# Gate copies on ScalarE, six PSUM banks for the second mixer, an MLP input scaled by ScalarE, and a later head norm

## The chip, the core and the metric

The kernel runs on one core of a Trainium2 chip. Its engines are TensorE (PE: matmuls and their weight loads), VectorE (DVE), ScalarE (ACT), GpSimd (POOL) and SyncE (SP, which issues the large DMAs). Each runs its own instructions in order and waits for others by semaphores. Operands lie in SBUF; matmul results go to PSUM, eight banks of 128 x 512 float32, from where VectorE and ScalarE read them. The metric is the device time of one execution in microseconds; the time before is the median of three runs.

## The reference

x has 256 tokens of width 1024. Three layers follow each other, each a mixer and a feed-forward part, all with an RMS norm ahead and a residual behind:

```
layer 0: x += even_mix(norm(x));  x += peer_ffn(norm(x))
layer 1: x += fox_mix(norm(x));   x += peer_ffn(norm(x))
layer 2: x += mix2(norm(x));      x += conv_gated_mlp(norm(x))
```

- peer_ffn: from q = h @ wq (8 heads, two halves of 128) the scores against 128 keys per half; the top 16 of each, the top 16 of their sums, a softmax over these. That makes 8 x 16 chosen experts out of 16384 for each token, each with a gate. act = gelu(h . u[expert]); the result is the sum of gate * act * v[expert].
- fox_mix: causal attention of 16 heads with normed q and k and a learned forget bias; o @ w_out.
- mix2: windowed attention of 8 heads with sinks, beside a spatial gating branch; both gated by sigmoids, merged and projected.
- conv_gated_mlp: z = h @ w_up, a causal convolution of three taps over the tokens, (silu(gate) * val) @ w_down.

## The kernel before, in words

Activations are kept transposed (128 features x 256 tokens, eight such blocks in xT). Each float32 weight block of 128 x 1024 comes by one DMA (w_raw), is rounded by ScalarE (`w_hi`, L337, in `Stream._hi`) and its rest is made by VectorE (`w_lo` = w_raw - w_hi, L353, in `Stream._split`). `mm3` (L454) makes one product out of three matmuls: hi x hi, hi x lo and lo x hi. Every block of work asks for its weights with `st.get()`, which also splits the block that stands two further on (look=2): so w_hi and w_lo of a later block stand in the program right ahead of the work that follows on the present one.

The expert layers (`peer`, twice) treat all 16384 experts densely in 128 blocks c of 128 experts. For each c: 24 matmuls make the up product in a PSUM bank (`pu`), ScalarE applies Gelu into a large tile X (L1271). In the same loop the gates are built (`gates`), four tokens at a step (GT = 4, so 64 steps), as a background generator that gets a turn after each block. One step s consists of

- `onehots(s)`: ScalarE makes a one-hot of the first key (four Abs, L1168, and a Relu, L1174), VectorE one of the second key and three products of it with parts of the gate (L1170, L1173);
- `products(s-1)`: twelve small matmuls into one PSUM bank `g`; two banks (2 and 3) take turns;
- `put(s-2)`: the gates of four tokens are brought into X. Blocks that have their activations already (c below `done["c"]`) are multiplied (L1190, two instructions, as X is two tiles), the others just get the gate copied in (L1192). When an activation comes later, ScalarE writes Gelu to `gl` (L1274) for the tokens that have gates already, and VectorE multiplies it into X (L1275).

The order is fixed in the program: after block c's up product come the Gelu, then one gate step. The library that records the program adds the semaphore waits that the accesses of tiles need, per tile in SBUF and per bank in PSUM. Background turns are counted by constants and not by measured time. After the 128 blocks the down products (`pv`) follow, with X as the moving operand.

The attention layer (`odd`) projects q and k in sixteen blocks. `quad(b)` (L1516) norms two heads' q and k: sums of squares by small matmuls (`qn_ps`), reciprocal roots, a broadcast by TensorE (`qn_rb`), products on VectorE. The generators in `flow` move one step on after each projection. When the last quad has run, eight `pair_chain`s are queued, one for two heads: logits (`lg`), softmax, transposes (`pt`), the product with v (`po`), and a split into y_hi (ScalarE) and y_lo (VectorE), after which `ready` names the pair. `attend` puts a block of projection work between their steps: the eight blocks of v, then six row blocks of the output projection (`rows`, one for each ready pair), then the last two.

`banks(j, a, l, o)` says which PSUM banks the projections (pj) and the small products (pa) take in turn; `acc(i)` is bank 4 + i. `mix2` begins with six projections (k, v, four q), then the value accumulators `va` in banks 4 and 5.

In `mlp` the first six pairs of up projections use h = xT * gain without the norm's factor, which VectorE multiplies in behind them (`zi`); from i = 6 on they use `hn`, the fully normed input. `normed()` makes it, one of eight blocks k at a flow step: room = xT * rb * gain on POOL (L1749, L1750), hn_hi on ScalarE (L1752), hn_lo on POOL (L1754).

Of the kernel before, what the change touches and what calls it, by code (L numbers as in the profile page):

```python
# [15 lines left out]
AF = mybir.ActivationFunctionType  # L16
OP = mybir.AluOpType
# [361 lines left out]
def body(ctx: ExitStack, tc: tile.TileContext, a, out, phases=(0, 6)):  # L379
    nc = tc.nc  # L380
# [21 lines left out]
    def banks(j, a_, l=(0,), o=(0,)):  # L402
        pj.set(j)
        pa.set(a_)
        pl.set(l)
        po.set(o)
# [6 lines left out]
    xT = base.tile([P, KD, S], F32, name="xT")  # L413
# [13 lines left out]
    def col(name, i=0, n=1):  # L427
        at, w = COLS[name]
        assert i + n <= w
        return cols[:, at + i:at + i + n]  # L430
# [44 lines left out]
    rb = base.tile([P, S], F32, name="rb")  # L475
# [514 lines left out]
    def peer(l):  # L990
        banks((0, 1, 4, 5), (2, 3))
        with ExitStack() as es:
# [50 lines left out]
            room = X(0, KD)  # L1043
# [109 lines left out]
            GT = 4  # L1153
            def gates():
                full = [P, GT // 2, P, 2]

                def pairs(t):

                    return t.rearrange("p (a b) -> p a b", b=2).unsqueeze(2).to_broadcast(full)

                def onehots(t0):


                    o = [t[:, i] for t in [tp.tile([P, 2, GT * P], BF16, name=t, tag=t) for t in ("oa", "ob")]
                         for i in range(2)]
                    two = [t.rearrange("p (a n b) -> p a n b", a=GT // 2, b=2) for t in o[1:]]
                    for i in range(GT):
                        nc.scalar.activation(o[0][:, i * P:(i + 1) * P], iota, AF.Abs,  # L1168
                                             bias=ne1T[:, t0 + i:t0 + i + 1])
                    nc.vector.tensor_tensor(two[2], iota2.unsqueeze(1).to_broadcast(full), pairs(e2b[:, t0:t0 + GT]),  # L1170
                                            op=OP.is_equal)
                    for part in range(3):
                        nc.vector.tensor_tensor(two[part], two[2], pairs(g3[:, part, t0:t0 + GT]), op=OP.mult)  # L1173
                    nc.scalar.activation(o[0], o[0], AF.Relu, bias=1.0, scale=-1.0)  # L1174
                    return o

                def products(o):
                    g = pa("g")
                    for i in range(GT):
                        for part in range(3):  # L1180
                            w = o[1 + part].rearrange("p (a n b) -> p a n b", a=GT // 2, b=2)[:, i // 2, :, i % 2]
                            mm(g[:, i * P:(i + 1) * P], o[0][:, i * P:(i + 1) * P], w,
                               i + part == 0, i == GT - 1 and part == 2)
                    return g

                def put(t0, g):
                    gt = g.rearrange("p (t c) -> p c t", t=GT)
                    c = done["c"]
                    for lo, hi, x in spans(0, c):
                        nc.vector.tensor_mul(x[:, :, t0:t0 + GT], gt[:, lo:hi], x[:, :, t0:t0 + GT])  # L1190
                    for lo, hi, x in spans(c, NCH):
                        nc.vector.tensor_copy(x[:, :, t0:t0 + GT], gt[:, lo:hi])  # L1192
                    done["t"] = t0 + GT

                n = S // GT
                hot, prod = {}, {}
                for s in range(n + 2):
                    if s < n:
                        hot[s] = onehots(s * GT)
                    if 0 <= s - 1 < n:  # L1200
                        prod[s - 1] = products(hot.pop(s - 1))
                    if s - 2 >= 0:
                        put((s - 2) * GT, prod.pop(s - 2))
                    yield G_COST
# [221 lines left out]
    def odd():  # L1426
        banks((4, 5, 6, 7), (0, 1, 2, 3))
        with ExitStack() as es:
# [85 lines left out]
            ready = set()  # L1514

            def quad(b):  # L1516
                yield from rms_heads(lambda b: qk[:, b], qz, lambda b: sq[:, slot(b)], [b, 8 + b, b + 1, 9 + b], [gq, col("odk"), gq, col("odk")], tp, bd64)
                if b == 6:
                    preload(AF.Exp)
                    for bb in range(8):  # L1520
                        pending.append(pair_chain(bb, (2 * bb, 2 * bb + 1), tp, qz, qk[:, 8 + bb], y, bias,
                                                  lambda hd: [cq[:, tb, hd:hd + 1] for tb in range(2)],
                                                  lambda hd: None, lambda hd: hd * 64, vn, ready))
# [36 lines left out]


    def mix2():
        banks((4, 5, 6, 7), (0, 1, 2, 3))
        with ExitStack() as es:
            sp = es.enter_context(tc.tile_pool(name="m2", bufs=1))
            st.extend(sp, 2, 3, 46)
# [166 lines left out]
    def mlp():  # L1733
        banks((0, 1, 4, 5, 6, 7), (2, 3))
        with ExitStack() as es:
            sp = es.enter_context(tc.tile_pool(name="ml", bufs=1))
            st.extend(sp, 3, 3, 66)
            tp = es.enter_context(tc.tile_pool(name="ml_t", bufs=2))
            room = sp.tile([P, KD, S], F32, name="room")
            hn = (sp.tile([P, KD, S], F32R, name="hn_hi"), sp.tile([P, KD, S], F32R, name="hn_lo"))  # L1740
            m = (sp.tile([P, NFF, S], F32R, name="m_hi"), sp.tile([P, NFF, S], F32R, name="m_lo"))

            zz = {}

            def normed():

                for k in range(KD + 2):
                    if k < KD:
                        nc.gpsimd.tensor_tensor(room[:, k], xT[:, k], rb, op=OP.mult)  # L1749
                        nc.gpsimd.tensor_scalar(room[:, k], room[:, k], col("ffn2", k), None, op0=OP.mult)  # L1750
                    if 0 <= k - 1 < KD:
                        nc.scalar.activation(hn[0][:, k - 1], room[:, k - 1], AF.Copy)  # L1752
                    if k - 2 >= 0:
                        nc.gpsimd.tensor_tensor(hn[1][:, k - 2], room[:, k - 2], hn[0][:, k - 2].bitcast(F32),  # L1754
                                                op=OP.subtract)
                    yield

            def conv(i, e, ps, scaled):

                if scaled:  # L1760
                    zi = tp.tile([P, S], F32, name="zi", tag="zi", bufs=3)
                    nc.vector.tensor_mul(zi, ps[:, :S], rb)
                    ps = zi
                    yield
                b = i + e * NFF
                z = tp.tile([P, S], F32, name="z", tag="z", bufs=8)
                w = lambda j: col("cw2", 3 * b + j)
                nc.scalar.activation(z, ps[:, :S], AF.Identity, scale=w(2), bias=col("cb2", b))
                for j in (1, 0):
                    s = 2 - j  # L1770
                    nc.vector.scalar_tensor_tensor(z[:, s:], ps[:, :S - s], w(j), z[:, s:], op0=OP.mult, op1=OP.add)
                zz[i, e] = z
                if e:
                    flow.add(gated(i))

            def gated(i):
                sg = tp.tile([P, S], F32, name="sg", tag="sg", bufs=4)
                nc.scalar.activation(sg, zz.pop((i, 0)), AF.Silu)
                yield
                nc.vector.tensor_mul(sg, sg, zz.pop((i, 1)))  # L1780
                yield
                nc.scalar.activation(m[0][:, i], sg, AF.Copy)
                yield
                nc.vector.tensor_sub(m[1][:, i], sg, m[0][:, i].bitcast(F32))

            def up_out(i, e, ps):
                flow.add(conv(i, e, ps, i < 6))

            proj2(h, lambda e, ps: up_out(0, e, ps))
            for i in range(1, NFF):  # L1790
                for e in range(2):
                    ps = pj("up")
                    proj_t(h if i < 6 else hn, ps[:, :S], then=lambda i=i, e=e, ps=ps: up_out(i, e, ps))
                    if (i, e) == (1, 0):
                        flow.add(normed())
                    flow.step()
            flush()
            flow.drain()
            w = None
            for n in range(KD):  # L1800
                ps = pj("dn")
                for i in range(NFF):
                    f = n * NFF + i
                    if f % 8 == 0:
                        w = st.get()
                    mm3(ps[:, :S], [t[:, (f % 8) * P:(f % 8 + 1) * P] for t in w], [t[:, i] for t in m],
                        i == 0, i == NFF - 1)
                nc.vector.tensor_add(xT[:, n], xT[:, n], ps[:, :S])  # L1808
                nc.sync.dma_start(out[:, n], xT[:, n])
# [38 lines left out]
```

## Time and profile before

| | before |
|---|---|
| median of 3 runs (lowest, highest) | 2348.55 us (2344.61, 2349.74) |
| the profiled execution | 2352.38 us, span 2350.6 |
| TensorE busy | 2315.8 us (99%) |
| VectorE busy | 1723.3 us (73%) |
| ScalarE busy | 1357.8 us (58%) |
| POOL busy | 93.6 us (4%) |
| mean granted TensorE clock | 0.994 |

Stages by time: the even mixer to about 155 us, the first expert layer to 1010 (its gates from 372 to 605), attention to 1155, the second expert layer to 1995 (gates from 1354 to 1587), the second mixer to 2150, the MLP to the end. A timeline row gives start, length, engine, line, operation and tiles, and in brackets the engine's idle time before it with what ended it. Matmuls are pipelined: the next one starts 0.12 us after a 256-wide one, though each row is 0.28 long, so TensorE's lost time is read from the distance of starts. The other engines also start an instruction a little before the one ahead has ended. Times of single instructions come from one profiled execution.

### The profile page before, as it was taken

The page shows a single profiled execution, that of the slowest core. Times are in us where ns is not written, and L with a number is a line of the kernel's source. Part 1 is how long each engine was busy: PE and PEld are TensorE (multiplying, and loading weights), DVE is VectorE, ACT ScalarE, POOL GpSimd, SP SyncE. Part 2 cuts the span into 40 slices and gives each one's busy share as a digit, 9 for nine tenths or more (in the row PEclk, how much of TensorE's full clock was granted, in tenths as well). Part 3 has the DMA queues.
Part 4 walks back from the last instruction along what each step waited for, and adds up shares of the span by engine and source line. Part 5 has one row for each costly group of instructions (what it writes and reads, how often), then busy time and mean ns, then how long its engine had stood idle before and what let it go on. Part 6 is the DMA issues. An engine that isn't in the chain of part 4 may idle for free. (4 is left out here: it accounts for less than half of the span.)

```text
span 2350.6 us, 48812 instructions
## 1 busy us (share of the span) xinstructions
PE 2315.8 (99%) x19664; PEld 2268.3 (97%) x19664; DVE 1723.3 (73%) x3656; ACT 1357.8 (58%) x2480; POOL 93.6 (4%) x107
## 2 busy tenths in 40 slices
PE   8999999999999999999999999999999999999999
PEld 7889999999999999998899999999999999999999
DVE  6668999999755555566699899996555555667983
ACT  6226448888544444455564588884444445555762
POOL 4100000000000000010000000000000000002300
PEclk9899999999999999999999999999999999999999
DMA  6114654444555666553256544446556565645553
GB/s 214 54 63 163 193 185 156 149 145 140 174 185 185 206 186 184 178 193 117 89 165 190 186 145 147 144 142 188 185 185 206 185 185 161 210 137 177 181 182 123
DMA packets 106626, 386.82 MB, mean 165 GB/s; under 512 B 11959, under 2 KB 13272, under 8 KB 106016
## 3 DMA queue, kind: packets, MB, share of 16 engines
q1 hardware_dynamic: 104976, 377.99, 50.7%
q0 software_dynamic: 1136, 5.32, 0.7%
q8 instruction: 154, 2.52, 0.4%
q14 instruction: 72, 0.59, 0.1%
q10 hardware_dynamic: 288, 0.40, 0.1%
HBM read 383.40 MB, written 1.05 MB: 164 GB/s over the span
## 5 line engine op out<-in xcount | busy, mean ns | idle before, releaser
L353 DVE TENSOR_TENSOR w_lo<-w_raw,w_hi 128x1024 fp32r<-128x1024 f32 x710 | 866.4, 1224 | 383.9 <-ACT w_hi L337 382.3
L337 ACT ACTIVATE w_hi<-w_raw 128x1024 fp32r<-128x1024 f32 x710 | 745.6, 1054 | 432.6 <-PE pv L452 348.0
L452 PE MATMUL pu<-h_hi,w_hi 128*128 128x256 f32 x2048 | 586.9, 287 | 0.0
L452 PE MATMUL pu<-h_lo,w_hi 128*128 128x256 f32 x2048 | 575.2, 281 | 0.0
L452 PE MATMUL pu<-h_hi,w_lo 128*128 128x256 f32 x2048 | 574.5, 281 | 0.0
L452 PE MATMUL pv<-h_hi,w_hi 128*128 128x256 f32 x1888 | 530.4, 281 | 0.0
L452 PE MATMUL pv<-h_lo,w_hi 128*128 128x256 f32 x1888 | 530.4, 281 | 0.0
L452 PE MATMUL pv<-h_hi,w_lo 128*128 128x256 f32 x1888 | 530.4, 281 | 0.0
L452 PEld LDWEIGHTS pu<-h_lo,w_hi 128*128 128x128 f32 x2048 | 386.4, 189 | 0.0
L452 PEld LDWEIGHTS pu<-h_hi,w_lo 128*128 128x128 f32 x2048 | 385.8, 188 | 0.0
L452 PEld LDWEIGHTS pu<-h_hi,w_hi 128*128 128x128 f32 x2048 | 385.5, 188 | 0.0
L452 PEld LDWEIGHTS pv<-h_hi,w_lo 128*128 128x128 f32 x1888 | 355.8, 188 | 0.0
L452 PEld LDWEIGHTS pv<-h_lo,w_hi 128*128 128x128 f32 x1888 | 355.8, 188 | 0.0
L452 PEld LDWEIGHTS pv<-h_hi,w_hi 128*128 128x128 f32 x1888 | 355.8, 188 | 0.0
L1271 ACT ACTIVATE X<-pu 128x256 f32<-128x256 f32 (+31 forms) x228 | 74.1, 325 | 197.2 <-PE pu L452 197.1
L1168 ACT ACTIVATE oa<-cb,routed 128x128 bf16<-128x128 f32 x512 | 162.9, 398 | 0.0
L1173 DVE TENSOR_TENSOR ob<-ob,g 128x512 bf16<-128x512 bf16 x256 | 108.0, 422 | 4.4
L452 PEld LDWEIGHTS <-oa 128*128 128x128 bf16 x1536 | 90.2, 96 | 12.9 <-issue 5.3
L452 PE MATMUL g<-ob,oa 128*128 128x128 bf16 x1024 | 102.1, 219 | 0.0
L452 PE MATMUL g<-oa 128*128 128x128 bf16 x512 | 94.7, 219 | 0.3
L461 DVE TENSOR_TENSOR h_lo<-X,h_hi 128x512 fp32r<-128x512 f32 (+1 forms) x134 | 86.4, 653 | 2.1 <-ACT h_hi L460 1.9
L1174 ACT ACTIVATE oa<-oa 128x512 bf16<-128x512 bf16 x128 | 80.8, 631 | 4.1
(450 smaller groups left out, 4122.3 us busy)
## 6 DMA issues: line engine op xcount, KB each, us to landing
w_raw<-in_s_u SPq DMA_DIRECT2D x256, 512.0 KB, 3.6
w_raw<-in_s_v SPq DMA_DIRECT2D x256, 512.0 KB, 3.6
w_raw<-in_s_mix SPq DMA_DIRECT2D x46, 512.0 KB, 3.9
w_raw<-in_s_up SPq DMA_DIRECT2D x44, 512.0 KB, 4.3
w_raw<-in_s_wq SPq DMA_DIRECT2D x32, 512.0 KB, 3.7
w_raw<-in_s_odd SPq DMA_DIRECT2D x32, 512.0 KB, 4.0
w_raw<-in_s_even SPq DMA_DIRECT2D x28, 512.0 KB, 3.9
w_raw<-in_s_down SPq DMA_DIRECT2D x22, 512.0 KB, 4.2
```

What stands on the lines that cost most here:

```text
L337: self.nc.scalar.activation(hi, raw, AF.Copy)
L353: self.nc.vector.tensor_sub(lo, raw, hi.bitcast(F32))
L452: nc.tensor.matmul(o, l, r, start=start, stop=stop, skip_group_check=True)
L461: nc.vector.tensor_sub(lo, src, hi.bitcast(F32))
L1168: nc.scalar.activation(o[0][:, i * P:(i + 1) * P], iota, AF.Abs, bias=ne1T[:, t0 + i:t0 + i + 1])
L1173: nc.vector.tensor_tensor(two[part], two[2], pairs(g3[:, part, t0:t0 + GT]), op=OP.mult)
L1174: nc.scalar.activation(o[0], o[0], AF.Relu, bias=1.0, scale=-1.0)
L1271: nc.scalar.activation(X(c)[:, td:], ps[:, td:S], AF.Gelu)
```

## The change

```diff
@@ gates().put, in peer @@
                     for lo, hi, x in spans(c, NCH):
-                        nc.vector.tensor_copy(x[:, :, t0:t0 + GT], gt[:, lo:hi])
+                        nc.scalar.activation(x[:, :, t0:t0 + GT], gt[:, lo:hi], AF.Copy)
@@ odd @@
             def quad(b):
+                yield
                 yield from rms_heads(lambda b: qk[:, b], qz, lambda b: sq[:, slot(b)], [b, 8 + b, b + 1, 9 + b], [gq, col("odk"), gq, col("odk")], tp, bd64)
@@ mix2 @@
-        banks((4, 5, 6, 7), (0, 1, 2, 3))
+        banks((4, 5, 6, 7, 0, 1), (2, 3))
@@ mlp, normed() @@
                     if k < KD:
-                        nc.gpsimd.tensor_tensor(room[:, k], xT[:, k], rb, op=OP.mult)
-                        nc.gpsimd.tensor_scalar(room[:, k], room[:, k], col("ffn2", k), None, op0=OP.mult)
+                        nc.scalar.activation(room[:, k], xT[:, k], AF.Copy, scale=col("ffn2", k))
+                        nc.gpsimd.tensor_tensor(room[:, k], room[:, k], rb, op=OP.mult)
```

The gate copies go from VectorE to ScalarE; the multiplications of the same step stay on VectorE and read the same PSUM bank. The head norm of each quad starts one flow step later. The second mixer's projections take six banks in turn and its small products two. The MLP's input gets its gain from ScalarE, and POOL multiplies by rb only.

ScalarE in one step of the gate stage of the first expert layer, with the semaphore of the engine that each waits for in brackets (DMAHW is a weight transfer). Before:

```order
L337 ACTIVATE w_hi<-w_raw 128x1024 [waits DMAHW3_49]
L1271 ACTIVATE X_1484<-pu 128x144 [waits PE_49]
L1274 ACTIVATE gl<-pu 128x112 [waits DVE_49]
L1168 ACTIVATE oa<-cb,routed 128x128 [waits DVE_49]
L1168 ACTIVATE oa<-cb,routed 128x128 x3
L1174 ACTIVATE oa<-oa 128x512 [waits Activation_49]
L337 ACTIVATE w_hi<-w_raw 128x1024 [waits DMAHW4_49]
```

ScalarE at the same place, after:

```order
L1192 ACTIVATE X_1484<-g 128x49x4 [waits DVE_49]
L337 ACTIVATE w_hi<-w_raw 128x1024 [waits DMAHW4_49]
L1271 ACTIVATE X_1484<-pu 128x140 [waits PE_49]
L1274 ACTIVATE gl<-pu 128x116
L1168 ACTIVATE oa<-cb,routed 128x128 x4
L1174 ACTIVATE oa<-oa 128x512 [waits Activation_49]
L1192 ACTIVATE X_1484<-g 128x48x4 [waits DVE_49]
```

The copy L1192 stands between the Relu of its step and the w_hi of the next block. In the built program the value that it waits for is reached by the second L1190 of the same step.

VectorE in the same step (the two X are the two tiles of X), before:

```order
L1190 TENSOR_TENSOR X_1483<-g,X_1483 128x44x4
L1190 TENSOR_TENSOR X_1484<-g,X_1484 128x35x4
L1192 COPY X_1484<-g 128x49x4
L353 TENSOR_TENSOR w_lo<-w_raw,w_hi 128x1024 [waits DMAHW4_49,PE_49,Activation_49]
L1275 TENSOR_TENSOR X_1484<-X_1484,gl 128x116 [waits DVE_49,Activation_49]
L1170 TENSOR_TENSOR ob<-iota_1490,e2b 128x512 [waits PE_49]
```

VectorE in the same step, after:

```order
L1190 TENSOR_TENSOR X_1483<-g,X_1483 128x44x4
L1190 TENSOR_TENSOR X_1484<-g,X_1484 128x35x4
L353 TENSOR_TENSOR w_lo<-w_raw,w_hi 128x1024 [waits DMAHW4_49,PE_49,Activation_49]
L1275 TENSOR_TENSOR X_1484<-X_1484,gl 128x116 [waits Activation_49]
L1170 TENSOR_TENSOR ob<-iota_1490,e2b 128x512 [waits PE_49]
```

Only the copy is gone; w_lo still waits for ScalarE's w_hi.

TensorE in the attention layer, where a row block of the output projection begins behind the logits of two heads. Before:

```order
L1392 MATMUL pt<-cb,pb 128x128
L452 MATMUL lg<-qk,qz 128x256
L452 MATMUL lg<-qk,qz 128x128
L452 MATMUL lg<-nck,sel 128x384
L452 LDWEIGHTS identb
L452 MATMUL lg<-causalb,identb 128x256
L452 MATMUL rows_13627<-y_hi,w_hi 128x256
L452 MATMUL rows_13627<-y_lo,w_hi 128x256
```

TensorE at the same place, after:

```order
L1392 MATMUL pt<-cb,pb 128x128
L452 MATMUL lg<-qk,qz 128x256
L452 MATMUL lg<-qk,qz 128x128
L452 MATMUL lg<-nck,sel 128x384
L452 LDWEIGHTS identb
L452 MATMUL lg<-causalb,identb 128x256
L452 MATMUL rows_13574<-y_hi,w_hi 128x256 [waits Activation_49]
L452 MATMUL rows_13574<-y_lo,w_hi 128x256 [waits DVE_49]
```

The row block now takes the pair whose y was split in the same slot; before it took a pair whose split lies a slot further back.

## Rows read from the trace of the kernel before

**Rows 1.** The page: busy us (share of the span) and instructions of each engine.

```profile
PE 2315.8 (99%) x19664; PEld 2268.3 (97%) x19664; DVE 1723.3 (73%) x3656; ACT 1357.8 (58%) x2480; POOL 93.6 (4%) x107
```

**Rows 2.** Windows: stretch, length, busy per engine (instructions), granted clock, DMA share, GB/s.

```profile
58.80:117.50 58.70, 54.36 (x341) 50.40 (x340) 40.83 (x91) 13.28 (x23) 8.28 (x8) 0.83 0.18 54
117.50:176.30 58.80, 54.46 (x369) 50.33 (x369) 37.33 (x77) 16.68 (x33) 1.47 (x2) 1.00 0.19 63
411.40:470.10 58.70, 58.70 (x585) 57.72 (x585) 57.61 (x147) 51.34 (x130) 0.00 (x0) 1.00 0.48 149
999.00:1057.80 58.80, 56.96 (x469) 56.00 (x468) 36.80 (x67) 35.02 (x59) 6.58 (x8) 0.97 0.54 193
```

**Rows 3.** Timeline of VectorE: one gate step early in the stage, one late.

```profile
386.53 1.23 DVE L353 TENSOR_TENSOR w_lo<-w_raw,w_hi 128x1024 fp32r<-128x1024 f32 x1
...
389.34 0.44 DVE L1190 TENSOR_TENSOR X<-g,X 128x176 f32<-128x176 f32 x2
...
390.13 1.23 DVE L353 TENSOR_TENSOR w_lo<-w_raw,w_hi 128x1024 fp32r<-128x1024 f32 x1
...
561.74 1.22 DVE L353 TENSOR_TENSOR w_lo<-w_raw,w_hi 128x1024 fp32r<-128x1024 f32 x1
...
564.74 0.64 DVE L1190 TENSOR_TENSOR X<-g,X 128x176 f32<-128x176 f32 x2
565.30 0.26 DVE L1192 COPY X<-g 128x104 f32<-128x104 f32 x1
565.47 1.22 DVE L353 TENSOR_TENSOR w_lo<-w_raw,w_hi 128x1024 fp32r<-128x1024 f32 x1
```

**Rows 4.** Timeline of ScalarE in the same early step, and a Gelu late in the stage.

```profile
386.88 0.37 ACT L1271 ACTIVATE X<-pu 128x244 f32<-128x244 f32 x1 [0.38 <-PE pu L452]
...
388.51 0.63 ACT L1174 ACTIVATE oa<-oa 128x512 bf16<-128x512 bf16 x1
389.05 1.05 ACT L337 ACTIVATE w_hi<-w_raw 128x1024 fp32r<-128x1024 f32 x1
...
562.01 0.21 ACT L1271 ACTIVATE X<-pu 128x52 f32<-128x52 f32 x1 [0.51 <-PE pu L452]
```

**Rows 5.** Timeline of TensorE where a gate product follows an up product.

```profile
565.43 0.28 PE L452 MATMUL pu<-h_hi,w_lo 128*128 128x256 f32 x1
565.70 0.22 PE L452 MATMUL g<-oa 128*128 128x128 bf16 x1
```

**Rows 6.** By line: copies (ns min/median/max, starts, forms); Abs (busy us, mean ns, idle).

```profile
L1192 DVE COPY X<-g x128: 206/338/469, 378.9 to 1590.5; 128x308 f32<-128x308 f32 x2, 128x304 f32<-128x304 f32 x2, 128x300 f32<-128x300 f32 x2, 128x296 f32<-128x296 f32 x2
...
L1168 ACT ACTIVATE oa<-cb,routed 128x128 bf16<-128x128 f32 x512 | 162.9, 398 | 0.0
```

**Rows 7.** Timeline: VectorE hands over to ScalarE, and ScalarE to VectorE.

```profile
2141.23 0.43 DVE L1704 TENSOR_TENSOR gt<-gt 128x256 f32<-128x256 f32 x1
...
2141.69 0.42 ACT L460 ACTIVATE y_hi<-gt 128x256 fp32r<-128x256 f32 x1 [1.28 <-DVE gt L1704]
...
2142.14 0.43 DVE L461 TENSOR_TENSOR y_lo<-gt,y_hi 128x256 fp32r<-128x256 f32 x1 [0.48 <-ACT y_hi L460]
```

**Rows 8.** Timeline of one slot of the attention layer.

```profile
1118.67 0.28 PE L452 MATMUL lg<-causalb,identb 128*128 128x256 bf16 x1
...
1119.41 0.38 ACT L460 ACTIVATE y_hi<-po 128x256 fp32r<-128x256 f32 x1
...
1119.83 0.42 DVE L461 TENSOR_TENSOR y_lo<-po,y_hi 128x256 fp32r<-128x256 f32 x1 [1.13 <-ACT y_hi L460]
```

**Rows 9.** Waits of TensorE: for whom, us in total, times, longest.

```profile
PE va L452 <- DVE gt L1599: 1.6, 1, 1.6
PE qn_ps L452 <- ACT qk_sq L1527: 1.6, 1, 1.6
...
PE up L452 <- DVE w_lo L353: 1.4, 1, 1.4
PE up L452 <- POOL hn_lo L1754: 1.3, 2, 1.0
```

## The prediction

> **What bounds the kernel now.** I read the busy shares first. TensorE is busy for 2315.8 of 2350.6 us [rows 1], so time can be won or lost only where TensorE waits, or where another engine's loop becomes longer than TensorE's. Then I read the stretches one by one. In the two stages in which gates are built, VectorE is busy for 57.61 of 58.70 us and ScalarE for 51.34 [rows 2]: all three engines are nearly full, and 128 steps (two layers of 64) run in this state.
>
> One such step is then read from the timelines. Each takes one 128-expert block of the up product on TensorE, and the gates of four tokens. Early in the stage VectorE starts its weight rest (w_lo) at 386.53 and again at 390.13, a period of 3.60 us; late in it at 561.74 and 565.47, 3.73 us [rows 3]. ScalarE has 0.38 us of idle time early and 0.51 late in each step, always while it waits for the up product [rows 4]. Late in the stage the gate product on TensorE starts at 565.70, and the VectorE copy that frees its bank ended at 565.30 + 0.26 = 565.56: TensorE waits for that copy. The matmul before it started at 565.43 and could have been followed 0.12 later, so the wait is 0.15 us, and TensorE's own step is 3.73 - 0.15 = 3.58 us [rows 3, 5]. VectorE sets the pace, by little.
>
> The list of TensorE's waits, read last, holds one of 1.6 us at the start of the second mixer, one of 1.6 in the attention layer and 1.4 + 1.3 in the MLP [rows 9].
>
> **The gate copy.** The edit takes 128 copies (206 to 469 ns, median 338) off VectorE [rows 6] and puts 128 ScalarE activations in their place. What decides is where they stand. In the order shown with the change, the copy stands on ScalarE between the Relu of a step and the w_hi of the next block, and it waits for VectorE. The wait is for the second multiplication (L1190) of the same step, the last VectorE work on that bank: after the change the gl and Abs activations name no VectorE wait any more, because this later one covers them. So the copy can start only when VectorE has ended the step's multiplications; the next w_hi is queued behind the copy; and VectorE's next instruction, w_lo, waits for that w_hi. Before, ScalarE made w_hi while VectorE was still busy with gates. Now one waits for the other in every step: multiplications, copy, w_hi, w_lo, one-hots, multiplications.
>
> The new step is this chain.
> - VectorE from the start of w_lo to the end of the multiplications: early 389.34 + 0.44 - 386.53 = 3.25 us, late 564.74 + 0.64 - 561.74 = 3.64 us [rows 3].
> - The copy on ScalarE is not in the trace. The nearest rows are Gelus from PSUM to the same tile: 0.37 us for 244 elements, 0.21 for 52, so 0.83 ns an element [rows 4]. 296 elements early cost 0.41 us, 104 late 0.25. Both ends: never under the 0.21 of the shortest Gelu; at most as dear per element as the Abs with its 398 ns for 128 [rows 6], that is 0.18 us more at the mean size of 182.
> - w_hi takes 1.05 us and starts 0.09 before the instruction ahead of it ends (389.05 against 388.51 + 0.63) [rows 4].
> - Two hand-overs, VectorE to ScalarE and back, at 0.03 us each: 2141.66 to 2141.69 and 2142.11 to 2142.14 [rows 7].
>
> Early: 3.25 + 0.03 + 0.41 - 0.09 + 1.05 + 0.03 = 4.68 us against 3.60. Late: 3.64 + 0.03 + 0.25 - 0.09 + 1.05 + 0.03 = 4.91 against 3.73. The step grows by 1.08 and 1.18, on the mean 1.13; 128 x 1.13 = 145 us. The rest of ScalarE's step hides: Gelu, Abs and Relu run beside w_lo and the one-hots. TensorE's 3.58 us fit into 4.7, and it idles for over a microsecond a step. The weights are split two blocks ahead, so the loss isn't caught up later: the blocks after the gates are bound by TensorE. Bounds: 128 x 0.18 = 23 us more with the dear copy, 128 x 0.11 = 14 less with 0.21 for every copy; hand-overs of 0.1 us would add 18.
>
> [...] No row of before shows the two engines in one bank at once.
>
> **The attention layer.** The extra yield puts each quad's norm one projection later. The 1.6 us wait for the squares goes [rows 9]. The stretch 999.00 to 1057.80 shows a mean clock of 0.97, and so does the slice after it: 0.03 x 58.8 = 1.8 us lost in each at the lower level, which may or may not come back; I take half of the 3.5. Against this, all pairs start one slot later, and each of six row blocks of the output projection now stands right behind its own pair, with waits for ScalarE and VectorE that it didn't have. In a slot of before the last logits matmul starts at 1118.67 and the pair's y_lo ends at 1119.83 + 0.42 = 1120.25; less 0.12 for that matmul it is 1.46 us of waiting, six times 8.8 us [rows 8]. Sum: 8.8 - 1.6 - 1.7 = +5.5 us, bounds 0 (slots that now overlap better, both clock losses back) and +9.
>
> **Second mixer.** With six banks the value accumulators no longer follow the last two queries into banks 4 and 5: the wait of 1.6 us goes [rows 9]. Two banks instead of four for the small products cost nothing, as whole projections lie between their uses. -1.6, bounds -1.8 and 0.
>
> **MLP input.** POOL loses eight of its 24 instructions, ScalarE gains eight scalings (0.4 to 0.5 us as its other 256-wide rows, hidden in its idle time). The waits for hn_lo and for w_lo, 1.3 + 1.4 us, go [rows 9]. -2.7, bounds -4 and +2 (ScalarE late with w_hi).
>
> Sum: 145 + 5.5 - 1.6 - 2.7 = +146.2 us on a profiled execution of 2352.4 us, so 2498.6. That execution was 3.8 us above the median of the runs, 2348.55; I predict 2494 us for the median.
>
> **Rivals.**
> 1. Faster: the copy doesn't hold ScalarE up. Place: ScalarE's idle time before each Gelu, 0.38 to 0.51 us [rows 4]. It decides if waiting and copying fit into that gap. Then VectorE's copies are gone and TensorE's own 3.58 us set the step: 0 to 0.15 us better, mean 0.08, 10 us; 2348.6 - 10 + 5.5 - 4.3 = 2340. Against it: early in the stage the Relu ends at 389.14 and the multiplications at 389.78 [rows 3, 4], so the wait alone is 0.64 us, above the gap of 0.38.
> 2. Slower, by half: the wait is there, but w_lo is ready ahead in time, and only the Gelu behind copy and w_hi holds VectorE up (its product with X needs it). Then w_lo's 1.23 us [rows 3] falls out of the chain and the two Gelus, about 0.58 us [rows 4], come into it: 1.13 - 1.23 + 0.58 = 0.48 us a step instead of 1.13, 61 us; 2348.6 + 61 + 1 = 2411. Against it: VectorE runs in order, and w_lo stands ahead of that product.
> [...]
>
> [...]
>
> **Chances.** My forecast 0.88, the rivals 0.04 each. The forecast's own range comes from the copy (-14, +23), the hand-overs (+18) and the small parts (about -7, +7): as a root of squares 30 us upwards and 16 downwards, and downwards 10 more, as the first and last steps of a stage, where part of the work is missing, may lose less: 2468 to 2524. I leave the rivals out of it, since they hold 0.12. About 0.2%, 4.7 us, can be told from no change here: faster 0.04, within 0.2% 0.01, slower 0.95.
>
> **What would show it.** In the profile of the changed kernel: the gate stages 70 us longer each; VectorE's w_lo waiting for ScalarE's w_hi once a step; ScalarE's L1192 waiting for VectorE's L1190; TensorE idle for about 1.1 us before each gate product, at full clock; TensorE waiting for y_hi and y_lo in the attention layer, and not for hn_lo in the MLP. A gate step below 3.7 us, or a copy that starts before the multiplications end, would prove the forecast wrong.

## The result, and the profile after

| | before | after |
|---|---|---|
| median of four runs each (lowest, highest) | 2348.82 us (2344.61, 2349.74) | 2491.64 us (2489.13, 2493.43) |
| profiled execution, span | 2350.6 us | 2487.3 us |
| mean granted TensorE clock | 0.994 | 0.999 |

The change makes the kernel slower: ratio 1.0611, 95% interval 1.0593 to 1.0629, that is 143 us. The forecast was 2494.

The page after, to be held against [rows 1]:

```profile
PE 2318.8 (93%) x19664; PEld 2268.7 (91%) x19664; DVE 1698.3 (68%) x3528; ACT 1387.3 (56%) x2616; POOL 82.8 (3%) x99
```

TensorE has as many matmuls as before and is as long busy with them; only its share fell, from 99 to 93%. VectorE lost 128 instructions and ScalarE gained 136, as the diff says. So the time is in waits, and the windows say in which stage. First the first expert layer's up product with its gates, before and after, then the same slice of 58.7 us as in [rows 2], after (columns as there):

```profile
229.20:646.60 417.40, 417.24 (x3849) 410.73 (x3848) 384.65 (x1014) 295.73 (x654) 0.00 (x0) 1.00 0.52 162
```

```profile
223.30:711.20 487.90, 421.94 (x3849) 414.77 (x3848) 373.07 (x950) 309.06 (x718) 0.00 (x0) 1.00 0.45 139
...
411.40:470.10 58.70, 46.72 (x454) 45.38 (x452) 40.55 (x98) 43.18 (x115) 0.00 (x0) 1.00 0.35 109
```

The stage grew by 70.5 us, with the same matmuls. The second expert layer's, started at 1211.2 before and at 1280.4 after, grew by 70.5 too: 141 us in all, nearly the whole difference. In the slice all three engines were nearly full before; now none is, and TensorE idles for a fifth of it. They wait for one another in a ring, which the list of waits shows (for whom, us in total, times, longest):

```profile
DVE w_lo L353 <- ACT w_hi L337: 555.2, 447, 5.5
...
ACT X L1192 <- DVE X L1190: 180.0, 128, 1.9
...
PE g L452 <- ACT X L1192: 131.9, 122, 1.2
```

The second row has one wait for each of the 128 gate copies, the third one for 122 of the 128 gate products, and the first has 125 more than the 322 of before. Here is the ring in one early step, by the timelines of VectorE, ScalarE and TensorE:

```profile
388.54 1.23 DVE L353 TENSOR_TENSOR w_lo<-w_raw,w_hi 128x1024 fp32r<-128x1024 f32 x1 [1.43 <-ACT w_hi L337]
...
391.36 0.44 DVE L1190 TENSOR_TENSOR X<-g,X 128x176 f32<-128x176 f32 x2
393.23 1.23 DVE L353 TENSOR_TENSOR w_lo<-w_raw,w_hi 128x1024 fp32r<-128x1024 f32 x1 [1.43 <-ACT w_hi L337]
```

```profile
390.03 0.63 ACT L1174 ACTIVATE oa<-oa 128x512 bf16<-128x512 bf16 x1
391.84 0.41 ACT L1192 ACTIVATE X<-g 128x292 f32<-128x292 f32 x1 [1.18 <-DVE X L1190]
392.15 1.05 ACT L337 ACTIVATE w_hi<-w_raw 128x1024 fp32r<-128x1024 f32 x1
```

```profile
392.30 0.22 PE L452 MATMUL g<-oa 128*128 128x128 bf16 x1 [0.95 <-ACT X L1192]
```

It reads as one chain without a gap. VectorE ends the multiplications at 391.36 + 0.44 = 391.80; ScalarE, idle for 1.18 us, starts the copy at 391.84; w_hi follows at 392.15 and ends at 393.20; VectorE, idle for 1.43 us, starts w_lo at 393.23. From w_lo to w_lo it is 4.69 us; [rows 3] had 3.60 there. TensorE's gate product starts 0.05 us after the copy's end and waits for it.

Late in the stage the chain is the same, with longer multiplications and a shorter copy:

```profile
614.34 1.23 DVE L353 TENSOR_TENSOR w_lo<-w_raw,w_hi 128x1024 fp32r<-128x1024 f32 x1 [1.27 <-ACT w_hi L337]
...
617.35 0.64 DVE L1190 TENSOR_TENSOR X<-g,X 128x176 f32<-128x176 f32 x2
619.26 1.22 DVE L353 TENSOR_TENSOR w_lo<-w_raw,w_hi 128x1024 fp32r<-128x1024 f32 x1 [1.27 <-ACT w_hi L337]
```

```profile
618.03 0.26 ACT L1192 ACTIVATE X<-g 128x104 f32<-128x104 f32 x1 [1.57 <-DVE X L1190]
618.18 1.05 ACT L337 ACTIVATE w_hi<-w_raw 128x1024 fp32r<-128x1024 f32 x1
```

4.92 us, against 3.73 in [rows 3].

The other stages, by the starts of TensorE's work: attention 144.2 to 148.5 us, the second mixer 159.2 to 157.4, the MLP 195.0 to 193.9. The even mixer ahead of them, which no edit touches, began its last matmul at 169.1 us instead of 175.2 in this execution (175, and not the "about 155" of the stages by time given ahead). The windows of before and after show why:

```profile
0.00:175.30 175.30, 155.53 (x1009) 142.41 (x1009) 115.47 (x227) 65.27 (x111) 36.42 (x45) 0.94 0.33 111
```

```profile
0.00:175.30 175.30, 155.85 (x1060) 142.84 (x1060) 120.77 (x237) 69.27 (x120) 40.28 (x48) 0.98 0.33 111
```

The granted clock was at its lower level for less of it (that level is 0.50: in the 10 us from 100.00 of this stage before, TensorE ran 46 matmuls, and 85 after, at 1.00). That goes by the execution and not by the kernel: over the ten traces of this study that last matmul began between 168.9 and 175.2 us, and in the kernel with two copies below, which has all of the change's edits, at 175.2; the kernel before alone ran at mean clocks of 0.993 to 0.998 in 25 executions. It explains why the spans differ by 136.7 us and the medians by 143.

### The profile page after: what moved, and what is told of

It is laid out like the page before. It is cut to its first block, busy times and chain, and to the rows that moved or that the text cites. A ratio compares the mean times of both kernels' runs of the same rounds, so it can differ in the third digit from the quotient of the medians.

```text
span 2487.3 us, 48681 instructions
## 1 busy us (share of the span) xinstructions
PE 2318.8 (93%) x19664; PEld 2268.7 (91%) x19664; DVE 1698.3 (68%) x3528; ACT 1387.3 (56%) x2616; POOL 82.8 (3%) x99
## 5 line engine op out<-in xcount | busy, mean ns | idle before, releaser
L452 PEld LDWEIGHTS <-oa 128*128 128x128 bf16 x1536 | 98.2, 96 | 145.9 <-issue 140.1
L1192 ACT ACTIVATE X<-g 128x308 f32<-128x308 f32 (+42 forms) x128 | 41.2, 322 | 180.0 <-DVE X L1190 180.0
```

The source lines that it names most:

```text
L452: nc.tensor.matmul(o, l, r, start=start, stop=stop, skip_group_check=True)
L1192: nc.scalar.activation(x[:, :, t0:t0 + GT], gt[:, lo:hi], AF.Copy)
```

## The experiments

In the order in which they ran. The first four ask which edit costs the time, and whether it is the copy's place.

**One edit alone.** The kernel before, with only the gate copies on ScalarE:

```diff
-                        nc.vector.tensor_copy(x[:, :, t0:t0 + GT], gt[:, lo:hi])
+                        nc.scalar.activation(x[:, :, t0:t0 + GT], gt[:, lo:hi], AF.Copy)
```

> Only the gate copy goes to ScalarE, the three small edits are left out. Theory (the copy waits for the multiplications of its step, with the next w_hi queued behind it): both stages of up product and gates 488 us as in the changed kernel (417 before), so 2490 us, 2485 to 2494. Rival (the small edits carry part of the 143 us, by TensorE's clock or the attention layer's waits): under 2470.

Measured: 2490.3 us, ratio 1.0604 (1.0581 to 1.0627), with stages of 487.9 us each in its trace, as in the changed kernel. This line is the whole loss.

**The other edits alone.** The changed kernel, with that line put back:

```diff
-                        nc.scalar.activation(x[:, :, t0:t0 + GT], gt[:, lo:hi], AF.Copy)
+                        nc.vector.tensor_copy(x[:, :, t0:t0 + GT], gt[:, lo:hi])
```

> The three small edits alone, gates copied by VectorE as before. Theory: the changed kernel's trace has the attention layer 4.3 us longer than before, the second mixer 1.8 and the MLP 1.1 shorter, so 2348.8 + 1.4 = 2350 us, 2345 to 2355, and up-product stages of 417. Rival (the small edits cost as much as predicted for the attention layer and gain nothing): 2354 or more; rival (they carry part of the 143): over 2370.

Measured: 2348.3 us, ratio 1.0003 (0.9991 to 1.0015). The three small edits together can't be told from nothing.

**The copy ahead of the multiplications.** The changed kernel, with two loops in `put` exchanged:

```diff
-                    for lo, hi, x in spans(0, c):
-                        nc.vector.tensor_mul(x[:, :, t0:t0 + GT], gt[:, lo:hi], x[:, :, t0:t0 + GT])
                     for lo, hi, x in spans(c, NCH):
                         nc.scalar.activation(x[:, :, t0:t0 + GT], gt[:, lo:hi], AF.Copy)
+                    for lo, hi, x in spans(0, c):
+                        nc.vector.tensor_mul(x[:, :, t0:t0 + GT], gt[:, lo:hi], x[:, :, t0:t0 + GT])
```

> The changed kernel with the two loops of put exchanged: the copy is written ahead of the multiplications, so the multiplications wait for the copy and not the other way. Same instructions on the same engines. Theory (the place behind the wait is the price, not the load on ScalarE): the copy starts right after the Relu, the step falls back to 3.6 to 3.7 us, the stages to 415 (412 to 422), the time to 2348 us, 2340 to 2358. Rival (ScalarE is full and each copy's 0.33 us lengthens the step): 128 x 0.33 = 42 over the small-edits kernel, about 2392. Rival (two engines reading one bank in turn cost the hand-over either way): 2430 or more.

Measured: 2344.6 us, ratio 0.9989 (0.9979 to 1.0000). The same instructions on the same engines, in another order, are 147 us faster. ScalarE and then VectorE in an early step (the copy is now L1190, the multiplications L1192):

```profile
392.33 0.63 ACT L1174 ACTIVATE oa<-oa 128x512 bf16<-128x512 bf16 x1
392.87 0.39 ACT L1190 ACTIVATE X<-g 128x288 f32<-128x288 f32 x1
393.16 1.05 ACT L337 ACTIVATE w_hi<-w_raw 128x1024 fp32r<-128x1024 f32 x1
```

```profile
390.65 1.23 DVE L353 TENSOR_TENSOR w_lo<-w_raw,w_hi 128x1024 fp32r<-128x1024 f32 x1 [0.34 <-ACT w_hi L337]
...
393.47 0.45 DVE L1192 TENSOR_TENSOR X<-g,X 128x176 f32<-128x176 f32 x2
394.24 1.23 DVE L353 TENSOR_TENSOR w_lo<-w_raw,w_hi 128x1024 fp32r<-128x1024 f32 x1 [0.32 <-ACT w_hi L337]
```

The gate product that ScalarE copies was made in an earlier step, and the copy starts without idle time before it. It is over at 393.26, before VectorE reaches the bank at 393.47. This step is 3.59 us, and TensorE, full in the whole stage (414.90 us busy of 414.90, against 417.24 of 417.40 before), sets it. Late in the stage a step is 3.64 to 3.71 us: there the multiplications have grown to 0.67 us, and VectorE has hardly any idle time left either (busy for 39.31 of the 40 us from 560 to 600).

**The copy behind the next w_hi.** The changed kernel, with each copy kept in a list and issued after the next block's weight split:

```diff
+                    late.extend((x[:, :, t0:t0 + GT], gt[:, lo:hi]) for lo, hi, x in spans(c, NCH))
...
                 proj_t(h, ps[:, :S])
+                copies()
```

> The changed kernel with the copy held back until the next block's w_hi has been issued: it still waits for the same multiplications, but no w_hi is queued behind it. Theory (what costs is w_hi behind the waiting copy): the chain closes over two steps instead of one, stages of 420 (415 to 428) and 2355 us, 2345 to 2372. Rival (the wait itself is the price, wherever w_hi stands): no change against 2492.

Measured: 2349.0 us, ratio 1.0008 (0.9997 to 1.0018). The copy still follows the multiplications, but w_hi now stands ahead of it. ScalarE and then VectorE in an early step (the copy is L1158, the multiplications L1197):

```profile
390.25 1.04 ACT L337 ACTIVATE w_hi<-w_raw 128x1024 fp32r<-128x1024 f32 x1
391.20 0.39 ACT L1158 ACTIVATE X<-g 128x288 f32<-128x288 f32 x1
```

```profile
390.52 0.45 DVE L1197 TENSOR_TENSOR X<-g,X 128x176 f32<-128x176 f32 x2
391.33 1.23 DVE L353 TENSOR_TENSOR w_lo<-w_raw,w_hi 128x1024 fp32r<-128x1024 f32 x1 [0.36 <-ACT w_hi L337]
```

While ScalarE makes w_hi, VectorE ends the multiplications, at 390.97, so the copy finds its bank free. In the whole trace ScalarE sat idle for the multiplications ahead of 2 of the 128 copies, 0.7 us in all, against 180.0 in the changed kernel. So the order, multiplications and then copy, costs next to nothing by itself (the stages are 2 us longer than with the copy ahead); the wait with w_hi queued behind it is what costs 70 us a stage. What ScalarE's wait would cost with nothing urgent behind it isn't shown, since hardly any wait is left. The middle of what was expected lay 6 us higher; the stage takes 417.0 us, 417.4 before, so nothing of that came.

The second four measure the copy's share, the bank's part, and the attention layer.

**Two copies.** The changed kernel:

```diff
-                    for lo, hi, x in spans(c, NCH):
+                    for lo, hi, x in 2 * list(spans(c, NCH)):
```

> The changed kernel, with each gate copy issued twice in a row on ScalarE (the same values are written again). Theory: the copy stands on the chain that sets the gate step, so a second one lengthens each of the 128 steps by a copy's own duration, 0.41 us early in the stage and 0.25 late, 0.33 on the mean: 42 us, 2491.6 + 42 = 2534 (2520 to 2545). Rival (ScalarE has idle time for it and something else sets the step): 2492.

Measured: 2535.3 us, ratio 1.0801 (1.0783 to 1.0820): 43.6 us more, 0.34 us a step. ScalarE in an early step:

```profile
394.48 0.86 ACT L1192 ACTIVATE X<-g 128x296 f32<-128x296 f32 x2 [1.16 <-DVE X L1190]
395.24 1.05 ACT L337 ACTIVATE w_hi<-w_raw 128x1024 fp32r<-128x1024 f32 x1
```

The pair takes 0.86 us where one took 0.41 to 0.42, w_hi comes later by as much, and so does the step. The copy's whole duration stands on the chain.

**Two banks.** The changed kernel, with every gate product written twice, and the copies reading the second one:

```diff
-                    g = pa("g")
-                    for i in range(GT):
+                    gg = [pa("g"), acc(2 + done["t"] // GT % 2, "g2")]
+                    for g in gg:
+                        for i in range(GT):
...
-                        nc.scalar.activation(x[:, :, t0:t0 + GT], gt[:, lo:hi], AF.Copy)
+                        nc.scalar.activation(x[:, :, t0:t0 + GT], gt2[:, lo:hi], AF.Copy)
```

> The changed kernel, with each gate product written twice by TensorE: into its usual bank, which VectorE's multiplications read, and into one of two banks not used in this stage, which ScalarE's copy reads. The copy stands at the same place in ScalarE's program, behind the multiplications in the code, but shares no bank with them. Theory (the shared bank makes the copy wait): ScalarE no longer waits for VectorE, and TensorE sets the step with 3.58 us plus twelve more matmuls, 3.58 - 24 x 0.119 = 0.72 us: 4.30 us instead of 3.60, 128 x 0.70 = 90 us above the kernel with the copy ahead of the multiplications (2344.6), 2435 (2420 to 2450). Rival (the step is longer because ScalarE has more to do, not because of the bank): the step keeps its 4.7 to 4.9 us or adds the 0.72, 2492 to 2584.

Measured: 2434.0 us, ratio 1.0370 (1.0352 to 1.0388). More matmuls made the kernel 58 us faster. The copy (L1193) and the multiplications (L1191), on ScalarE and VectorE:

```profile
393.55 0.40 ACT L1193 ACTIVATE X<-g 128x292 f32<-128x292 f32 x1
393.85 1.05 ACT L337 ACTIVATE w_hi<-w_raw 128x1024 fp32r<-128x1024 f32 x1
```

```profile
390.64 1.23 DVE L353 TENSOR_TENSOR w_lo<-w_raw,w_hi 128x1024 fp32r<-128x1024 f32 x1 [0.96 <-ACT w_hi L337]
...
393.54 0.44 DVE L1191 TENSOR_TENSOR X<-g,X 128x176 f32<-128x176 f32 x2
394.93 1.23 DVE L353 TENSOR_TENSOR w_lo<-w_raw,w_hi 128x1024 fp32r<-128x1024 f32 x1 [0.95 <-ACT w_hi L337]
```

They start 0.01 us apart and read different banks at the same time, at their usual 0.40 and 0.44 us. The copy stands in the same place of the program as in the changed kernel and waits for nothing: it was the shared bank that made it wait, and not the tile of X, into which the copy and the second multiplication still both write. The step is 4.29 us, TensorE's own with twelve more matmuls (459.00 us busy of 460.90). No run here has both engines in one bank without an order between them.

**Without the yield.** The kernel with the copy ahead, less one line of the attention layer:

```diff
             def quad(b):
-                yield
```

> The kernel with the copies ahead of the multiplications (0.9989 of the time before), without the extra yield in the attention layer; the six banks and the scaled MLP input stay. Theory: the yield costs the 4.3 us that the attention stage grew by in the trace, so 2344.6 - 4.3 = 2340.3, ratio 0.9970 (0.996 to 0.998). Rival (the growth is given back in the work after it, or only the profiled execution had it): 2344.6, ratio 0.9989.

Measured: 2341.3 us, ratio 0.9972 (0.9961 to 0.9984). It is close to the ratio that the theory gave, 0.9970, but the interval overlaps that of the kernel with the yield (0.9979 to 1.0000): by the time alone the yield's cost is likely, not shown. In the traces the attention layer takes 144.0 us here and 148.3 with the yield.

**Row blocks one slot later.** The kernel with the copy ahead and the yield:

```diff
-                attend(rows.add if rows.n in ready else None, pending, ready)
+                attend(rows.add if rows.n + 1 in ready else None, pending, ready)
```

> The kernel with the copies ahead of the multiplications, with the yield, but each of the six row blocks of the attention layer's output projection is issued only when the pair after its own is ready, one slot later. Theory: the six waits of 1.39 us for y_hi and y_lo go, 8.3 us, and one slot without a row block between the pairs costs up to 3: 2344.6 - 5 to 8 = 2338, ratio 0.996 (0.9950 to 0.9975). Rival (the waits only mark the pair's own chain, which then stalls the next logits or transposes instead): 2344.6 to 2348, ratio 0.9985 to 1.000.

Measured: 2335.4 us, ratio 0.9962 (0.9948 to 0.9976), the lowest of all; it beats both the kernel before and the changed one, while against the kernel without the yield the intervals overlap. First a row block of the changed kernel on TensorE, with the ScalarE and VectorE rows that it waits for, then one of this kernel on TensorE:

```profile
1167.70 0.28 PE L452 MATMUL lg<-causalb,identb 128*128 128x256 bf16 x1
1168.87 0.39 PE L452 MATMUL rows<-y_hi,w_hi 128*128 128x256 f32 x1 [0.89 <-ACT y_hi L460]
1169.33 0.39 PE L452 MATMUL rows<-y_lo,w_hi 128*128 128x256 f32 x1
...
1168.44 0.38 ACT L460 ACTIVATE y_hi<-po 128x256 fp32r<-128x256 f32 x1
...
1168.85 0.42 DVE L461 TENSOR_TENSOR y_lo<-po,y_hi 128x256 fp32r<-128x256 f32 x1 [1.13 <-ACT y_hi L460]
```

```profile
1100.63 0.28 PE L452 MATMUL lg<-causalb,identb 128*128 128x256 bf16 x1
1100.67 0.36 PE L452 MATMUL rows<-y_hi,w_hi 128*128 128x256 f32 x1
```

In the changed kernel 1.17 us pass from the last logits matmul to the row block, then 0.46 to its second matmul; less 0.12 for each it is 1.39 us, six times 8.3. Here the row block follows at once. Two new waits came, 1.4 us for y_lo ahead of a product with v and 1.0 ahead of a transpose, so part of the rival holds. The stage is 141.2 us, against 148.3 in the kernel with the copy ahead.

## Why the prediction was right

**The gate copy: 145 predicted, 141 measured.** All links of the chain came as summed. Early 4.69 us for the 4.68 forecast, late 4.92 for 4.91. The copy, which no row of before showed, took 0.41 us for 292 elements and 0.26 for 104, where 0.83 ns an element gave 0.41 and 0.25; its neighbour by kind, the Gelu of [rows 4], was the right row, and the Abs of [rows 6] wasn't. The hand-overs took 0.04 and 0.03, as in [rows 7]. The two copies confirm the term's size by itself, and the copy behind w_hi that the price is gone once w_hi no longer stands behind the copy. The 4 us that are missing are the first steps of each layer, as the range allowed for: the first two gate products of a layer follow one another in 3.60 and 3.68 us, with no chain yet.

**Rival 1, faster.** It needed waiting and copying to fit into ScalarE's idle time of 0.38 to 0.51 us. ScalarE waited 1.18 to 1.57 us for VectorE alone. Near the rival's 2340 the copy ahead of the multiplications ended up (2344.6), by the rival's own mechanism: the copy doesn't hold ScalarE up. But its price was too high. TensorE's 3.58 us don't set the late steps, which took 3.64 to 3.71; each gate stage became 2.4 us shorter, 4.9 in all, and not 10.

**Rival 2, w_lo ready ahead.** VectorE waits for w_hi 125 times more often, so w_lo stays on the chain.

**The granted clock.** The last 0.04 of the chances was for a lower one. In the window 223.30 to 711.20 it is 1.00, with TensorE idle for 1.1 us in each step. With two copies, where the waits are longer (up to 1.5 us), the mean of the whole execution is 0.996, against 0.994 before.

**The attention layer: +5.5 predicted, +4.3 in the trace.** The six waits came, 8.3 us for 8.8, and the wait for the squares [rows 9] went. The clock's loss came back wholly and not by half. The stretch of the q and k projections, first without the yield, then in the kernel with the row blocks one slot later:

```profile
1006.50:1070.40 63.90, 62.09 (x502) 60.85 (x501) 38.21 (x74) 36.02 (x60) 7.62 (x9) 0.95 0.51 177
```

```profile
1002.10:1060.50 58.40, 58.22 (x498) 57.10 (x496) 37.67 (x71) 36.98 (x62) 7.62 (x8) 1.00 0.55 194
```

Every kernel with the yield has 58.4 to 58.9 us there, and the three without 63.9 to 66.9, with the wait in the stretch and the clock at its lower level for part of it. 8.8 - 1.6 - 3.5 would have been 3.7. The 4.3 compare two executions: in the kernel with one edit alone, which has no yield, the clock fell for longer, and the layer took 147.1 us. What is steady is the part behind the q and k projections, from the first matmul of the v projection on: 80.0 to 80.1 us in the three traces without the yield and 89.1 to 89.2 in the six with it and with the row blocks as in the change. The kernel with the row blocks one slot later has both: the clock and no waits of the row blocks.

**Second mixer: -1.6 predicted, -1.8 measured.** The wait for the gate tile [rows 9] is gone, and nothing took its place.

**MLP: -2.7 predicted, -1.1 in the trace.** Of the two waits in [rows 9] the 1.3 us for hn_lo went; the one for w_lo, 1.4 us, did not: it is 2.1 us in two places now. I had counted it as POOL's doing, to go with POOL's eight instructions. POOL, VectorE and TensorE around the longer one, after:

```profile
2325.31 1.78 POOL L1755 TENSOR_TENSOR hn_lo<-room,hn_hi 128x256 fp32r<-128x256 f32 x2
```

```profile
2318.72 0.41 DVE L1781 TENSOR_TENSOR sg<-sg,z 128x256 f32<-128x256 f32 x1
...
2325.55 0.95 DVE L1781 TENSOR_TENSOR sg<-sg,z 128x256 f32<-128x256 f32 x1
2326.43 0.41 DVE L1763 TENSOR_TENSOR zi<-up,rb 128x256 f32<-128x256 f32 x1
2326.76 1.42 DVE L353 TENSOR_TENSOR w_lo<-w_raw,w_hi 128x1024 fp32r<-128x1024 f32 x1
```

```profile
2328.23 0.38 PE L452 MATMUL up<-hn_hi,w_lo 128*128 128x256 f32 x1 [1.64 <-DVE w_lo L353]
```

The same product on VectorE takes 0.41 us while POOL is idle and 0.95 beside POOL's hn_lo. The product zi, which reads one of its inputs from PSUM, keeps its 0.41 beside the same POOL rows. POOL works less than before, but what is left of it still stands beside the VectorE rows ahead of that w_lo. This is read from rows; no run took POOL's last instructions away. Nor are the -1.1 a firm size: the MLP takes 195.0 us in both traces without this edit and 193.8 to 195.3, 194.5 on the mean, in the eight with it. The waits for w_lo come to 2.0 to 3.0 us in these, and the two waits of before came to 2.7. So this edit gained about half a microsecond, and the step that failed is the 1.4 us for w_lo, counted as gone.

**The sum.** 141 + 4.3 - 1.8 - 1.1 = 142.4 us by stages; 142.8 between the medians; 146.2 forecast.

## What to carry to other kernels

Before work is moved to an engine with room, look at what it waits for there and what is queued behind it: here the wait was paid by the next instruction that another engine needs, w_hi, and a copy of 0.3 us on an engine busy for 58% cost 1.1 us a step. Where two engines read one PSUM bank, look at the program's order between them as at any other dependency (ScalarE waited 180.0 us in all for it): let the one that is ready early read first (2344.6 us here, against 2491.6), give them separate banks (2434.0, with twelve more matmuls a step), or put nothing urgent behind the second (2349.0). Each of the six row blocks released by its own pair's last step waited 1.39 us for it; releasing them one slot later took those waits away.

## What the runs showed of the hardware

- ScalarE's copy from PSUM into a strided tile took 0.41 us for 292 elements a partition and 0.26 for 104, so 0.8 ns an element above some 0.18 us. Two in a row take 0.86, no less than twice one.
- In the changed kernel TensorE idled for over a microsecond in each step of 4.7 us, for 300 us on end, and the granted clock of the window 223.30 to 711.20 was 1.00. In the q and k stretch a single wait of 1.6 us was followed by stretches at the lower level, in all three traces that have it: the stretch has a mean of 0.95 in the kernel before and in the one without the yield, and 0.92 in the kernel with one edit alone. The length of a wait alone didn't decide it: waits for w_lo in the MLP, of 1.4 us before and 1.6 after, were followed by none (1.00 from 2185.00 to 2290.00 before, and from 2325.00 to 2430.00 after).
- The time of one kernel went with the mean granted clock of the execution: the kernel before took 2343.4 to 2353.5 us in 25 executions, at 0.998 and 0.993, and the fastest kernel ran in 2335.3 us at 0.999 and in 2343.9 at 0.995.
- VectorE's product of two SBUF tiles (`sg`) took 0.41 us with POOL idle and 0.95 beside POOL's hn_lo, in the trace after; `zi`, with one input in PSUM, took 0.41 beside it.
